# S5 maps: two products summed inside TensorE instead of on VectorE

## The chip, the cores and the metric

The kernel runs on one core of one Trainium2 chip. The metric is the device time of one execution in microseconds (us). The engines are TensorE (PE in the rows; its weight loads are PEld), VectorE (DVE), ScalarE (ACT), GpSimd (POOL) and the DMA queues, which SyncE (SP) issues for the most part. Each engine works through its own list of instructions in order and waits on semaphores for the others.

## The reference, cut to what matters

The program is one layer of an encoder: an S5 state-space mixer with GLU beside a cross-attention, an output projection with a layer norm, and a mixture of 16 experts. The change touches only the S5 mixer:

```
lam_bar = exp(lam * step)                                   # per direction, 32 groups x 64 states, complex
b_bar = ((lam_bar - 1.0) / lam)[..., None] * bmat
bu = einsum('blgc,gpc->blgp', ug, b_bar)                    # 16 channels of a group to 64 states
_, states = associative_scan(combine, (lam_bar, bu), reverse=(direction == 1), axis=1)
y = y + real(einsum('gcp,blgp->blgc', cmat, states))
```

The scan over 2048 steps is done in 128 chunks of 16 steps. For that the kernel needs, for each group and direction, an input map (16 steps x 16 channels to 64 complex states): its entries are real and imaginary parts of `lam_bar^k * b_bar`, k from 0 to 15, and an output map with `lam_bar^k * c`.

## The kernel before, in words

The part that matters runs from the start to about 333 us. In `inproj_u`, 16 tiles of 128 tokens are loaded and projected: for each tile t, `pu` (24 fp16 matmuls of 512 columns, the S5 input) and `pq` (48 fp16 matmuls of 128 columns, the query). Each of the two has one PSUM buffer; `pq` is read by ACT and DVE into `OT`. After the first tile, `s5_base` computes powers of `lam_bar` (`PR`, `PI`; `PRb` is the copy of `PR` in PSUM) and the products with b (`XB`, `YB`), mostly on DVE. `scan_base` builds a rotation table `E` on DVE and POOL. From tile 6 on, `s5_block(b)` makes the maps of 4 groups; there are 8 such blocks, and all of them come before the scans.

In `s5_block`, the helper `powers` makes one map of one direction from two products: POOL multiplies the imaginary parts into `wtmp` (two buffers), DVE multiplies the real parts into `wz` in PSUM (half a block at a time) and then adds both into `wi` (input map, one buffer) or `wo` (output map). The 16 tiles of `wi` in a block are transposed by TensorE with the identity into `ptw` (four to a PSUM tile, two tiles in rotation, shared with `ptu`), ACT copies them to `wt`, and a DMA stores `wt` in `wid`. After that `pkk` (fp32 matmuls of `wo` against `XB`) makes the convolution kernel `kd`. `ptu` are the transposes of the projected input into `U`.

At the end of the stage `chunk_inputs` multiplies `wt` and `U` (`pvv`) for the two last blocks, whose maps stay on the chip; ACT copies the result to `S`. Then `scan` turns the states (`m`, on DVE and POOL), scans them on DVE and turns them back, block by block, while `kv` prepares the cross-attention's keys. Later stages (attention, GLU, output projection, experts) are not touched.

No order is written out by hand here: a scheduler in the framework orders each engine's list from its own estimates, so an edit can also move instructions that it does not name. From `s5_out` on the order of TensorE alone is the one of the code. The lines to follow are 576 (POOL's product), 580 (DVE's product), 581 (DVE's sum), 600 (the transposes), 612 to 614 (`pkk`), 638 (`pvv`), 690 to 715 (the scan).

Of the kernel before, what the change touches and what calls it, by code (L numbers as in the profile page):

```python
# [9 lines left out]
F32 = mybir.dt.float32  # L10
# [3 lines left out]
ALU = mybir.AluOpType  # L14
# [4 lines left out]
P = 128  # L19
# [5 lines left out]
GB = 4  # L25
KEEP = 2
NB = G // GB
# [40 lines left out]
EPS2 = 1e-5 * GATE * GATE  # L68
EPS = 1e-5
MAGIC = 12582912.0  # L70


class Kern:
# [307 lines left out]
    def s5_base(self, t0):  # L381
# [13 lines left out]
        with ExitStack() as s:  # L395
# [9 lines left out]
            def ts(x, s1, op0, s2=None, op1=None, dt=F32):  # L405
                o = T("ts", dt)
                V.tensor_scalar(o, x, s1, s2, op0=op0, **({"op1": op1} if op1 is not None else {}))
                return o
# [13 lines left out]
            def rnd(x, k):  # L422
                return ts(ts(x, k, MUL, MAGIC, ADD), MAGIC, SUB)

# [126 lines left out]
    def s5_block(self, b, ps):  # L551
        nc = self.nc
        V, Q = nc.vector, nc.gpsimd
        bp = self.blkp
        gs = slice(b * GB, b * GB + GB)
        wo = bp.tile([P, GB, 2, 17, 16], F32, tag="wo", bufs=2, name=f"wo{b}")
        if b < NB - 1:
            wi = bp.tile([P, GB, 2, 16, 16], F32, tag="wi", bufs=1, name=f"wi{b}")
        else:
            wi = self.spare.rearrange("p a g d k -> p (a g d k)").rearrange("p (g d n c) -> p g d n c", g=GB, d=2, c=16)  # L560

        def pw(t, sl, d, q, n):
            t = t[:, sl, d, gs][:, :, q].rearrange("p n g -> p g n")
            return t.unsqueeze(3).to_broadcast([P, t.shape[1], n, 16])

        def ch(t, q, n):
            t = t[:, q]
            return t.unsqueeze(2).to_broadcast([P, t.shape[1], n, 16])


        def powers(o, x, y, d, n, back, nm):
            up = slice(n - 1, None, -1) if back else slice(0, n)
            lo = slice(n, 0, -1) if back else slice(1, n + 1)
            t = bp.tile([P, GB, 16, 16], F32, tag="wtmp", bufs=2, name=f"wtmp{nm}")
            all_ = slice(0, GB)
            Q.tensor_tensor(t[:, :, 0:n], ch(y, all_, n), pw(self.PI, lo, d, all_, n), op=ALU.mult)
            for h in range(2):
                q = slice(2 * h, 2 * h + 2)
                z = ps.tile([P, 2, 16, 16], F32, tag="wz", bufs=1, name=f"wz{nm}{h}")[:, :, 0:n]
                V.tensor_tensor(z, ch(x, q, n), pw(self.PRb, up, d, q, n), op=ALU.mult)  # L580
                V.tensor_tensor(o[:, q], z, t[:, q, 0:n], op=ALU.add)

        for d in range(2):
            o = wi[:, :, d]
            nc.scalar.activation(o[:, :, 15 if d == 0 else 0], self.XB[:, d, gs], AF.Copy)
            powers(o[:, :, 0:15] if d == 0 else o[:, :, 1:16], self.XB[:, d, gs], self.YB[:, d, gs], d, 15, d == 0, f"i{b}{d}")
        for d in range(2):
            o = wo[:, :, d]
            nc.scalar.activation(o[:, :, 16 if d == 0 else 0], self.XC[:, gs], AF.Copy)
            powers(o[:, :, 0:16] if d == 0 else o[:, :, 1:17], self.XC[:, gs], self.YC[:, gs], d, 16, d == 0, f"o{b}{d}")  # L590
        wof = wo.rearrange("p g d n c -> p g d (n c)")
        for d in range(2):
            nc.sync.dma_start(self.wod[b][:, :, d], wof[:, :, d, 16 * d:16 * d + 256])
        wt = bp.tile([P, GB, 2, 2, P], F32, tag="wt", bufs=2, name=f"wt{b}")
        for g in range(GB):
            pt = ps.tile([P, 512], F32, tag="tr", bufs=2, name=f"ptw{b}{g}")
            for d in range(2):
                for J in range(2):
                    q = d * 2 + J
                    nc.tensor.transpose(pt[:, q * P:q * P + P], wi[:, g, d, 8 * J:8 * J + 8].rearrange("p j c -> p (j c)"), self.ident)  # L600
            nc.scalar.activation(wt[:, g].rearrange("p d j s -> p (d j s)"), pt, AF.Copy)
        if b < NB - KEEP:
            nc.sync.dma_start(self.wid[b], wt)

        pk = ps.tile([P, 512], F32, tag="pk", bufs=1, name=f"pkk{b}")
        for g in range(GB):
            r = slice(g * 32, g * 32 + 32)
            gi = b * GB + g
            lf = self.XB[:, 0, gi:gi + 2, :].rearrange("p g c -> p (g c)")
            lb = self.XB[:, 1, gi:gi + 2, :].rearrange("p g c -> p (g c)")  # L610
            tp = (0, g * 32)
            nc.tensor.matmul(pk[r, 0:256], lf, wof[:, g, 0, 16:272], start=True, stop=False, tile_position=tp)
            nc.tensor.matmul(pk[r, 240:256], lb, wof[:, g, 1, 0:16], start=False, stop=True, tile_position=tp)
            nc.tensor.matmul(pk[r, 256:496], lb, wof[:, g, 1, 16:256], start=True, stop=True, tile_position=tp)
        ks = bp.tile([P, TAU * 16], F32, tag="ks", bufs=1, name=f"ks{b}")
        nc.scalar.activation(ks, pk[:, :496], AF.Copy)
        V.tensor_tensor(ks[:, 240:256], ks[:, 240:256], self.Dd[:, b], op=ALU.add)
        for g in range(GB):
            nc.sync.dma_start(self.kd[b][:, g], ks[g * 32:g * 32 + 16])
        return wt  # L620
# [547 lines left out]
    def list_row(self, kp, pos, e, out, shape, nm):  # L1168
# [3 lines left out]
        V.tensor_scalar(c, pos, 1.0 / P, -0.5 + 1.0 / 256, op0=ALU.mult, op1=ALU.add)  # L1172
        V.tensor_scalar(c, c, MAGIC, MAGIC, op0=ALU.add, op1=ALU.subtract)
        q = kp.tile([P] + shape, F32, tag=f"lr_q{shape[0]}", name=f"lrq{nm}")
# [6 lines left out]
    def overflow_tiles(self, c, n, nm):  # L1181
# [4 lines left out]
        V.tensor_scalar(nov, nov, 1.0 / OVT, (OVT - 1.0) / OVT - 0.5 + 1.0 / (2 * OVT), op0=ALU.mult, op1=ALU.add)  # L1186
        V.tensor_scalar(nov, nov, MAGIC, MAGIC, op0=ALU.add, op1=ALU.subtract)
        one = T([NE], "one")
# [414 lines left out]
```

## Time and profile before

| what | value |
|---|---|
| median of 3 runs | 1094.92 us (1094.09 to 1098.54) |
| the profiled execution | 1094.93 us, of which the span of its instructions is 1093.1 us |
| busy share of the span | PE 82%, DVE 79%, POOL 52%, ACT 49% |
| mean granted clock of TensorE | 0.927 of full speed |

The span runs from the first to the last instruction; 1.83 us of the profiled execution lie around it. Busy time of PE overlaps: a matmul is shown until its result has drained, while the next one already runs, so what a matmul costs in a row of equal ones is the distance from start to start. The chain that ended last covers only the last 12 us and says nothing of this stage.

### The profile page before, as it was taken

What the parts mean: (1) busy time and instruction counts of PE and PEld (TensorE: products, weight loads), DVE (VectorE), ACT (ScalarE), POOL (GpSimd) and SP (SyncE); (2) the same over time, 40 slices, a digit from 0 to 9 for tenths busy, and PEclk for the clock granted to TensorE, in tenths of its full rate; (3) what the DMA queues carried; (4) which work ended last, traced back from release to release, by engine and by line L of the source; (5) the groups of instructions that cost most, each with busy time, mean ns of one, the idle gap of its engine ahead of it and who ended that gap; (6) DMA issues with size and microseconds to landing.
All of it is one profiled execution on the core that took longest, in us unless ns stands there. A gap on an engine that the chain in (4) does not pass through costs nothing. (4 is left out here: it accounts for less than half of the span.)

```text
span 1093.1 us, 18792 instructions
## 1 busy us (share of the span) xinstructions
PE 900.1 (82%) x7108; PEld 606.2 (55%) x7108; DVE 861.1 (79%) x1704; ACT 533.3 (49%) x1052; POOL 568.9 (52%) x403
## 2 busy tenths in 40 slices
PE   7678599986736998899999888698969996989880
PEld 4445455665625777444455447486647664756640
DVE  7999988869999878983585767478858796879774
ACT  5123243444836666677733312276536564656530
POOL 1475754336656557425935444524524556357454
PEclk9899899998977999999999887899989998999995
DMA  7113355274271340417745331586578669567531
GB/s 254 39 57 107 117 199 183 78 256 144 69 222 58 119 143 10 140 54 261 253 149 115 80 117 59 172 327 220 181 249 294 223 220 326 188 218 237 211 104 65
DMA packets 65197, 178.13 MB, mean 163 GB/s; under 512 B 15120, under 2 KB 33424, under 8 KB 57680
## 3 DMA queue, kind: packets, MB, share of 16 engines
q1 hardware_dynamic: 44800, 128.83, 35.7%
q0 software_dynamic: 20304, 48.07, 12.9%
q8 instruction: 57, 0.93, 0.4%
q14 instruction: 36, 0.29, 0.1%
HBM read 141.95 MB, written 58.49 MB: 183 GB/s over the span
## 5 line engine op out<-in xcount | busy, mean ns | idle before, releaser
L92 DVE SCALAR_TENSOR_TENSOR wl<-raw,wh 128x1024 f16<-128x1024 f32 x82 | 97.7, 1217 | 9.7 <-ACT wh L91 9.7
L91 ACT ACTIVATE wh<-raw 128x1024 f16<-128x1024 f32 x82 | 81.9, 1048 | 24.3 <-PE pg L109 13.5
L109 PE MATMUL pg<-xl,wh 128*128 128x288 f16 (+1 forms) x256 | 72.9, 287 | 3.7 <-DVE xl L1473 3.6
L1217 POOL DMA_INDIRECT xs<-xg,idxall x31 | 40.8, 1317 | 67.3 <-DVE xg L1510 40.2
L108 PE MATMUL pg<-xh,wh 128*128 128x288 f16 (+1 forms) x256 | 73.1, 288 | 0.0
L110 PE MATMUL pg<-xh,wl 128*128 128x288 f16 (+1 forms) x256 | 72.7, 287 | 0.0
L108 PE MATMUL pu<-xh,wh 128*128 128x288 f16 (+1 forms) x256 | 71.3, 281 | 1.7 <-DVE hl L1060 1.7
L109 PE MATMUL pu<-xl,wh 128*128 128x288 f16 (+1 forms) x256 | 71.2, 281 | 0.0
L110 PE MATMUL pu<-xh,wl 128*128 128x288 f16 (+1 forms) x256 | 71.1, 281 | 0.0
L110 PEld LDWEIGHTS <-wl 128*128 128x128 f16 x576 | 57.7, 100 | 17.7 <-issue 4.5
L109 PEld LDWEIGHTS <-wh 128*128 128x128 f16 x576 | 57.8, 100 | 17.2 <-issue 3.8
L108 PEld LDWEIGHTS <-wh 128*128 128x128 f16 x576 | 58.0, 101 | 15.7 <-issue 0.9
L108 PE MATMUL pq<-xh,S 128*128 128x128 f16 x256 | 49.7, 232 | 17.8 <-DVE OT L295 17.8
L108 PE MATMUL py<-wh,hh 128*128 128x512 f16 x120 | 45.9, 385 | 14.0 <-DVE xg L1510 9.9
L108 PE MATMUL pu<-winh,xh 128*128 128x512 f16 x128 | 49.7, 389 | 6.8 <-ACT winh L91 6.8
L691 POOL TENSOR_TENSOR m<-S,R 128x1024 f32<-128x1024 f32 x10 | 33.0, 3301 | 42.4 <-DVE S L715 24.1
L1212 POOL DMA_INDIRECT xg<-x1d,idxall x31 | 36.9, 1191 | 32.9 <-DMA out_x<-xg,idxall 11.9
L1469 PE MATMUL pt<-ident,xg 128*128 128x128 f32 x240 | 37.9, 286 | 17.3 <-DVE xl L1473 7.9
L1473 DVE TENSOR_TENSOR xl<-pt,xh 128x512 f16<-128x512 f32 x60 | 39.5, 682 | 14.9 <-ACT xh L1472 14.9
L109 PE MATMUL pu<-winl,xh 128*128 128x512 f16 x128 | 49.7, 388 | 0.1
L1472 ACT ACTIVATE xh<-pt 128x512 f16<-128x512 f32 x60 | 33.9, 592 | 32.4 <-PE pt L1469 32.4
L110 PE MATMUL pq<-xh,S 128*128 128x128 f16 x256 | 49.7, 232 | 0.0
(476 smaller groups left out, 3205.6 us busy)
## 6 DMA issues: line engine op xcount, KB each, us to landing
raw<-in_w_gate SPq DMA_DIRECT2D x16, 1024.0 KB
raw<-in_w_up SPq DMA_DIRECT2D x16, 1024.0 KB
raw<-in_w_down SPq DMA_DIRECT2D x16, 1024.0 KB
xr<-in_xT SPq DMA_DIRECT2D x16, 512.0 KB
xs<-wo SPq DMA_DIRECT2D x16, 512.0 KB
wol<-xs SPq DMA_DIRECT2D x16, 512.0 KB
M<-kd SPq DMA_DIRECT2D x64, 128.0 KB
xres<-in_x SPq DMA_DIRECT2D x16, 512.0 KB
```

Of the source, the lines that this page charges most:

```text
L91: self.nc.scalar.activation(hi, raw, AF.Copy, scale=WS)
L92: self.nc.vector.scalar_tensor_tensor(lo, raw, WS, hi, op0=ALU.mult, op1=ALU.subtract)
L108: mm(ps, lh, rh, start=first, stop=False)
L109: mm(ps, lh, rl, start=False, stop=False)
L110: mm(ps, ll, rh, start=False, stop=last)
L691: Q.tensor_tensor(m[:, 1], S[:, :, 1::-1], tab(1), op=ALU.mult)
L1212: return self.nc.gpsimd.indirect_dma_start(out=out, out_offset=None, in_=src, in_offset=bass.IndirectOffsetOnAxis(ap=idx, axis=0))
L1217: st = self.nc.gpsimd.indirect_dma_start(out=self.xs, out_offset=bass.IndirectOffsetOnAxis(ap=si, axis=0), in_=z[:sz], in_offset=None, bou ...
L1469: nc.tensor.transpose(pt[:, i, off:off + sz], x[:sz, (d0 + i) * P:(d0 + i) * P + P], self.ident[:sz, :sz])
L1472: nc.scalar.activation(xh[:, ds_, :n], pt, AF.Copy)
L1473: nc.vector.tensor_tensor(xl[:, ds_, :n], pt, xh[:, ds_, :n], op=ALU.subtract)
```

## The change

The sum on VectorE and `wz` go for the input map only. DVE now multiplies the real parts of a whole block and direction straight into `wi` (line 590 in the new file), POOL multiplies the imaginary parts into a second buffer, and TensorE transposes both and adds them in PSUM: two fp32 matmuls with the identity as the moving operand, the first with `start`, the second with `stop`, take the place of each transpose. For blocks 0 to 5 the second buffer is a part of `U[:, 1]`, which is free until the last tile; blocks 6 and 7 use `wtmp`. POOL's product has 16 steps instead of 15. The output map is made as before.

```diff
+WTB = 2
...
-        for d in range(2):
             o = wi[:, :, d]
             nc.scalar.activation(o[:, :, 15 if d == 0 else 0], self.XB[:, d, gs], AF.Copy)
-            powers(o[:, :, 0:15] if d == 0 else o[:, :, 1:16], self.XB[:, d, gs], self.YB[:, d, gs], d, 15, d == 0, f"i{b}{d}")
+            V.tensor_tensor(o[:, :, 0:15] if d == 0 else o[:, :, 1:16], ch(self.XB[:, d, gs], all_, 15),
+                            pw(self.PRb, slice(14, None, -1) if d == 0 else slice(0, 15), d, all_, 15), op=ALU.mult)
+            if b < NB - 2:
+                t = self.U[:, 1, (b % 2 * 2 + d) * 8:(b % 2 * 2 + d) * 8 + 8].rearrange("p (g n) (m c) -> p g (n m) c", g=GB, c=16)
+            else:
+                t = bp.tile([P, GB, 16, 16], F32, tag="wtmp", bufs=WTB, name=f"wtmpi{b}{d}")
+            Q.tensor_tensor(t, ch(self.YB[:, d, gs], all_, 16),
+                            pw(self.PI, slice(15, None, -1) if d == 0 else slice(0, 16), d, all_, 16), op=ALU.mult)
+            wti.append(t)
...
-                    nc.tensor.transpose(pt[:, q * P:q * P + P], wi[:, g, d, 8 * J:8 * J + 8].rearrange("p j c -> p (j c)"), self.ident)
+                    for k, w in enumerate((wi[:, g, d], wti[d][:, g])):
+                        nc.tensor.matmul(pt[:, q * P:q * P + P], w[:, 8 * J:8 * J + 8].rearrange("p j c -> p (j c)"), self.ident,
+                                         start=(k == 0), stop=(k == 1))
```

The scheduler's lists change with it. On PE, where block 0's input map is turned (inside `pu` of tile 6), before:

```order
L108 LDWEIGHTS xh_1243
L108 MATMUL pu_1249<-winh,xh_1243 128x512
L600 MATMUL ptw_686<-ident,wi_646 128x128 x2
L600 MATMUL ptw_692<-ident,wi_646 128x128 x2
L109 LDWEIGHTS xh_1243
L109 MATMUL pu_1249<-winl,xh_1243 128x512
```

and now (line numbers are higher by 1 to 15 in the new file):

```order
L111 LDWEIGHTS xl_1256
L111 MATMUL pu_1261<-winh,xl_1256 128x512
L614 MATMUL ptw_674<-ident,wi_646 128x128
L614 MATMUL ptw_674<-ident,U 128x128
...
L614 MATMUL ptw_684<-ident,wi_646 128x128
L614 MATMUL ptw_684<-ident,U 128x128
...
L627 MATMUL pkk_715<-wo_645,XB 32x256
L628 MATMUL pkk_715<-wo_645,XB 32x16
```

A run of 16 plain matmuls stands where 4 transposes stood, after the whole of `pu` instead of inside it. In all, the list has 256 `ptw` matmuls where there were 128. The maps of blocks 0 to 2 are now turned before `ptu` and tile 8, and those of block 3 right behind them.

On DVE, at block 0's input map and the start of its output map, before:

```order
L581 TENSOR_TENSOR wi_646<-wzi_650,wtmpi_648 128x2x240
L580 TENSOR_TENSOR wzi_653<-XB,PRb 128x2x240
L295 SCALAR_TENSOR_TENSOR OT<-pq_1104,OT 64x2x128
L581 TENSOR_TENSOR wi_646<-wzi_653,wtmpi_648 128x2x240
L262 TENSOR_TENSOR xl_1391<-xr_1247,xh_1390 128x1024
L657 TENSOR_TENSOR S<-E 128x64
L580 TENSOR_TENSOR wzi_659<-XB,PRb 128x2x240
```

and now:

```order
L590 TENSOR_TENSOR wi_646<-XB,PRb 128x4x240 x2
L582 TENSOR_TENSOR wzo_656<-XC,PRb 128x512
L263 TENSOR_TENSOR xl_1403<-xr_1259,xh_1402 128x1024
L296 SCALAR_TENSOR_TENSOR OT<-pq_1112,OT 64x2x128
L583 TENSOR_TENSOR wo_645<-wzo_656,wtmpo_654 128x2x256
L582 TENSOR_TENSOR wzo_659<-XC,PRb 128x512
```

Eight instructions of a block became two of twice the length, and no sum of the input map is left. At the start of the scans DVE had before:

```order
L349 TENSOR_TENSOR meml<-mraw_2843,memh 128x1024
L349 TENSOR_TENSOR meml<-mraw_2847,memh 128x1024
L690 TENSOR_TENSOR m_2774<-S,R_2775 128x1024
L695 TENSOR_TENSOR S<-m_2774 128x2x256 x2
L715 SCALAR_TENSOR_TENSOR S<-decay,S 128x128 x4
```

and has now:

```order
L705 TENSOR_TENSOR m_2810<-S,R_2811 128x1024
L710 TENSOR_TENSOR S<-m_2810 128x2x256 x2
L730 SCALAR_TENSOR_TENSOR S<-decay,S 128x128 x8
L350 TENSOR_TENSOR meml<-mraw_2879,memh 128x1024
L705 TENSOR_TENSOR m_2810<-S,R_2811 128x1024
L350 TENSOR_TENSOR meml<-mraw_2883,memh 128x1024
```

The two conversions of the memory tokens (`meml`) moved from ahead of the first scan to behind it.

## Rows read from the trace of the kernel before

**Rows 1.** Page, busy time by engine: us, share of the span, instructions.
```profile
PE 900.1 (82%) x7108; PEld 606.2 (55%) x7108; DVE 861.1 (79%) x1704; ACT 533.3 (49%) x1052; POOL 568.9 (52%) x403
```

**Rows 2.** Windows: stretch, its length, busy us of each engine, granted clock, DMA share.
```profile
74.00:140.00 66.00, 48.98 (x443) 34.12 (x441) 61.23 (x89) 20.04 (x47) 43.30 (x26) 0.90 0.34 118
120.00:130.00 10.00, 6.56 (x61) 4.92 (x62) 8.47 (x12) 0.78 (x3) 7.52 (x4) 0.60 0.48 159
140.00:224.00 84.00, 82.12 (x665) 50.81 (x664) 70.34 (x105) 36.43 (x81) 38.23 (x19) 1.00 0.43 142
233.00:333.00 100.00, 61.67 (x566) 49.35 (x563) 96.31 (x118) 51.66 (x119) 60.70 (x24) 0.83 0.52 156
74.00:233.00 159.00, 138.90 (x1236) 92.19 (x1233) 137.55 (x197) 60.61 (x132) 84.14 (x48) 0.96 0.42 144
```

**Rows 3.** Waits of PE from 74 to 233 us: total, times, longest.
```profile
PE pkk L614 <- DVE wo L581: 8.1, 2, 7.3
PE pq L108 <- DVE OT L295: 4.1, 3, 2.4
PE pkk L612 <- DVE wo L581: 2.5, 1, 2.5
PE ptw L600 <- DVE wi L581: 2.3, 2, 1.8
```

**Rows 4.** Groups by form on DVE and POOL: busy us, mean ns | idle before.
```profile
L580 DVE TENSOR_TENSOR wzo<-XC,PRb 128x512 f32<-128x512 f32 x32 | 22.2, 693 | 0.8
L580 DVE TENSOR_TENSOR wzi<-XB,PRb 128x480 f32<-128x480 f32 x32 | 21.1, 659 | 0.7
L581 DVE TENSOR_TENSOR wi<-wzi,wtmpi 128x480 f32<-128x480 f32 x28 | 18.4, 656 | 3.1 <-POOL wtmpi L576 1.8
L581 DVE TENSOR_TENSOR S<-wzi,wtmpi 128x480 f32<-128x480 f32 x4 | 2.6, 655 | 0.2
L576 POOL TENSOR_TENSOR wtmpo<-YC,PI 128x1024 f32<-128x1024 f32 x16 | 33.8, 2114 | 27.6 <-DVE wi L581 22.1 <-DVE ks L617 2.8 <-DVE S L581 2.7
L576 POOL TENSOR_TENSOR wtmpi<-YB,PI 128x960 f32<-128x960 f32 x16 | 31.8, 1988 | 19.5 <-DVE wo L581 19.5
```

**Rows 5.** Groups by form on PE, 74 to 233 us.
```profile
L612 PE MATMUL pkk<-wo,XB 128*32 128x256 f32 x64 | 19.4, 406 | 2.6 <-DVE wo L581 2.5
L600 PE MATMUL ptw<-ident,wi 128*128 128x128 f32 x112 | 17.1, 279 | 3.3 <-DVE wi L581 2.3 <-ACT wt L601 0.8 <-ACT U L306 0.2
L638 PE MATMUL pvv<-U,wt 128*64 128x128 f32 x128 | 7.4, 274 | 1.2 <-ACT S L641 1.2
L600 PE MATMUL ptw<-ident,S 128*128 128x128 f32 x16 | 2.1, 276 | 0.0
```

**Rows 6.** Timeline of PE: start, length in us, instruction.
```profile
166.58 1.04 PE L600 MATMUL ptw<-ident,wi 128*128 128x128 f32 x8
167.55 0.62 PE L612 MATMUL pkk<-wo,XB 128*32 128x256 f32 x2
...
293.27 0.59 PE L808 MATMUL py<-wol,SS 128*128 128x256 f32 x2
293.70 0.59 PE L809 MATMUL py<-wol,SS 128*128 128x256 f32 x2
...
660.76 1.93 PE L966 MATMUL pl<-wr,xT 128*128 128x20 f32 x16 [0.51 <-DVE lg L972]
```

**Rows 7.** Timeline of DVE at the start of the scans.
```profile
228.92 1.23 DVE L349 TENSOR_TENSOR meml<-mraw,memh 128x1024 f16<-128x1024 f32 x1
230.06 3.38 DVE L690 TENSOR_TENSOR m<-S,R 128x1024 f32<-128x1024 f32 x1
...
238.55 1.22 DVE L690 TENSOR_TENSOR m<-S,R 128x1024 f32<-128x1024 f32 x1
242.03 0.69 DVE L695 TENSOR_TENSOR S<-m 128x512 f32<-128x512 f32 x1 [2.25 <-POOL m L691]
243.88 1.23 DVE L690 TENSOR_TENSOR m<-S,R 128x1024 f32<-128x1024 f32 x1 [1.16 <-POOL S L695]
```

**Rows 8.** Timeline of ACT at the end of the stage.
```profile
228.79 1.07 ACT L641 ACTIVATE S<-pvv 128x512 f32<-128x512 f32 x2
```

More of the change, by code (lines that the diff above doesn't have):

```diff
@@ L560, in s5_block @@
             wi = self.spare.rearrange("p a g d k -> p (a g d k)").rearrange("p (g d n c) -> p g d n c", g=GB, d=2, c=16)
+        all_ = slice(0, GB)
         def pw(t, sl, d, q, n):
@@ L573, in powers @@
             lo = slice(n, 0, -1) if back else slice(1, n + 1)
-            t = bp.tile([P, GB, 16, 16], F32, tag="wtmp", bufs=2, name=f"wtmp{nm}")
-            all_ = slice(0, GB)
+            t = bp.tile([P, GB, 16, 16], F32, tag="wtmp", bufs=WTB, name=f"wtmp{nm}")
             Q.tensor_tensor(t[:, :, 0:n], ch(y, all_, n), pw(self.PI, lo, d, all_, n), op=ALU.mult)
@@ L581, in powers @@
                 V.tensor_tensor(o[:, q], z, t[:, q, 0:n], op=ALU.add)
+        wti = []
         for d in range(2):
```

## The prediction

> **What bounds the kernel now.** I read the page's busy shares first: PE 82% and DVE 79% of the span [rows 1] are two near-equal averages, and neither says who ends the stage that the change touches. The windows do. Between 74 and 140 us (tile 6 onwards, blocks 0 to 2, the rotation table) DVE is busy 61.2 of 66 us and PE 49.0; between 140 and 224 us (blocks 3 to 7, tiles 8 to 15) PE is busy 82.1 of 84 us and DVE 70.3; from 233 to 333 us (the scans) DVE is busy 96.3 of 100 us and PE 61.7 [rows 2]. So the limit changes hands twice: DVE, then PE, then DVE. What the change is worth is read between 74 us, where tile 6 begins on PE, and 233 us, where `pvv` of the two last blocks ends; the scans can't begin before `pvv`. In these 159 us PE works 138.9 us and stands idle 20.1 [rows 2]. 17.0 of the 20.1 are four waits for DVE: 8.1 and 2.5 us of `pkk` for `wo`, 4.1 of `pq` for `OT`, 2.3 of `ptw` for `wi` [rows 3]; a `pkk` wait of 7.3 us lies in the slow stretch around 120 us, where the granted clock was 0.60.
>
> **DVE's part.** Removed: 32 products of 480 elements at 659 ns and 32 sums at 656 ns (28 and 4), 21.1 + 18.4 + 2.6 = 42.1 us. Added: 16 products of 960. 480 elements take 659 ns and 512 take 693 [rows 4], 1.06 ns an element, so 960 take 0.659 + 480 x 1.06 ns = 1.17 us, 18.7 us in all. DVE saves 23.4 us, 2.9 us a block. It counts where PE waits for DVE, up to about 140 us, and nowhere behind that.
>
> **POOL's part.** 16 products grow from 1988 to the 2114 ns of the 1024-element form, +2.0 us [rows 4]. POOL has 43.3 of 66 and 38.2 of 84 us of work [rows 2], and its waits for DVE to release `wtmp` get fewer, since the input map of blocks 0 to 5 has buffers of its own in `U`. I cost it at nothing; POOL's 2 us is its price if that cover fails. ACT's and the DMA queue's work is the same in amount. Token loads now stand behind stores of earlier blocks on SP's queue, but blocks 0 to 3 themselves come earlier against the tiles, so the loads of tiles 9 and later, issued when those stores are ready, land tens of us before their tile: nothing.
>
> **PE's part, the term that decides.** Removed: 128 transposes (112 + 16 in rows 5). Eight in a row take 0.97 us from start to the next instruction's start [rows 6], 0.121 us each: 15.5 us. Added: 256 plain fp32 matmuls of 128 columns. The trace of before has this operation with other sizes, and its counts tell something that the code doesn't: the code issues 64 `pvv` matmuls for the two last blocks, 32 `pkk` matmuls of line 612 and 128 transposes, and the trace has 128, 64 and 128 of them [rows 5]. A plain fp32 matmul runs as two passes, a transpose as one. So 512 passes come in. What a pass costs is bounded by two rows: two `py` passes of 256 columns take 0.43 us from start to start, 0.84 ns a column, which makes 0.1075 us of 128; and the router's fp32 passes with a full 128x128 weight and only 20 columns still take 1.93 us for 16, 0.121 us each [rows 6], so loading an fp32 weight sets a floor of the same size, hidden behind the pass before it. I take 0.115 us: 58.9 us (55.0 to 62.0). Net on PE: +43.4 us (39.5 to 46.5).
>
> The Trainium skill, in "TensorE: Matmul & The Clock Gate", section Terms, says that the transpose mode is four times faster for FP32. By that a plain matmul would cost four transposes instead of the 1.9 (0.23 against 0.121 us) of these rows; what that would give is the third rival.
>
> **What lies beside other work.** The idle 20.1 us of PE are the only room. They shrink from both sides: a block's maps are ready 2.9 us earlier on DVE, and PE has 5.4 us more to do in each block (43.4 / 8), so a wait for `wo` of 7.3 us is closed by one block. But they don't go to zero. The scheduler now puts the maps of blocks 0 to 2 one behind the other into tiles 6 and 7, where PE has little else to do when DVE is late; and in blocks 6 and 7 POOL's products for both maps share the two `wtmp` buffers, which now stay taken until PE has turned the input map, so that POOL (2.1 us) and DVE (0.7 us each) come after it and before the last `pkk`, which stands ahead of `pvv`. A new wait of PE for DVE holds up `pq`, `pu` and with them everything behind. I leave 7 us of idle time (0 to 17): 13.1 us are recovered. The clock: a denser PE should not fall to 0.60 as between 120 and 130 us, where 6.6 us of work were done [rows 2]; at full clock that work is at best 3.3 us shorter; I take 2.
>
> **The start of the scans.** DVE begins at 230.06 us, 0.2 us after ACT has written `S` (228.79 + 1.07) [rows 7, 8]. It will begin right behind `S` again, that much later. The two `meml` (1.23 us each) were done before it for free and now fall behind the first scan, into waits of 2.25 and 1.16 us for POOL [rows 7]: they cost what they fill. In before they also stood ahead of `S` through ACT's part of them; I take 1 us of gain (0 to 1.5). After that DVE is the limit with the same work and everything later shifts as a whole.
>
> **The sum.** +43.4 (passes) - 13.1 (idle time filled) - 2 (clock) - 1 (start of the scans) = +27.3 us. Against the profiled execution, 1094.93 us (span 1093.1 and 1.83 around it), that is 1122 us; the median of the runs shown is 1094.92, so nothing is to be corrected. Lower end: 39.5 - 20.1 - 3.3 - 1.5 = +14.6, 1109.5 us. Upper end: 46.5 - 3.1 - 0 - 0 = +43.4, 1138 us.
>
> **Rivals.**
> 1. Faster or no change: PE takes the extra work within its waits, and DVE's 23.4 us decide. This needs one pass a matmul when the moving operand is the identity. Then 256 x 0.115 = 29.4 us come in, net +13.9; less 13.1 to 20.1 of idle time, 2 of clock and 1 of the scans, that is -2 to -9, 1086 to 1093 us. For it: DVE is the limit up to 140 us and gives up 2.9 us a block. Against it: all three plain fp32 groups have two records a matmul, whatever their operands. The point from which it decides: net cost on PE below 16 us, that is under 0.25 us for what one transpose did; I expect 0.46.
> 2. Much slower through waits: DVE and POOL can't feed PE in the early blocks, or the one buffer of `wi`, now held through 7.4 us of matmuls, makes DVE wait and then PE again for `OT`. Idle time stays at the 17 to 22 us of today: +43.4 - 3 to + 2, 1135 to 1140 us. For it: DVE is 93% busy in that stretch. Against it: DVE loses a fifth of its work there and PE gains it.
> 3. The passes cost four transposes: 256 x 0.484 = 124 us, net +108, less 20 of idle time and 3 of clock and scans: +85, 1180 us. Against it: every row of fp32 passes is at 0.11 to 0.12 us.
> 4. The shift is partly given back behind 233 us, by another order of the scans, the keys and the attention, which the scheduler also moved: 10 to 15 us less, 1107 to 1112 us. Against it: DVE is 96% busy there, with the same work.
>
> **Chances.** Forecast 80%, rival 1 6%, rival 2 8%, rival 3 2%, rival 4 4%. The forecast's own range is 1110 to 1135. For 8 in 10 I take 1108 to 1137, which holds rival 4 and half of rival 2 and leaves out rivals 1 and 3. About 0.5% (5.5 us) is what a measurement of this kernel can tell from no change. Rival 1 splits evenly between faster and the same, and a little more is left for an early stage that goes better than counted: faster 4%, same 5%, slower 91%.
>
> **What would show it.** Right: 512 records of `ptw` with some 0.115 us from start to start; `pvv` ending at 256 to 264 us instead of 233; PE busy above 95% of the time from 74 us on, and DVE at some 70%; DVE's groups of 480 elements replaced by 16 of 1.17 us; the distance from the first `m` to the end as before, within 5 us. Wrong: 256 records of `ptw`, or a pitch over 0.13 us; PE waiting more than 17 us for DVE before `pvv`; or `pvv` late by 25 us and the end not.

## The result and the profile after

The changed kernel takes 1134.24 us (1126.02 to 1136.3, 4 runs) against 1095.87 for the kernel before on the same chip (1094.09 to 1098.54): a ratio of 1.0336 [1.0297, 1.0375]. On a second chip it was 1.0350 [1.0307, 1.0393]. The forecast was 1122 us within 1108 to 1137: slower, inside the range near its upper end, and some 10 us short. The profiled execution has a span of 1130.6 us against 1093.1, +37.5 us, and these 37.5 are what the forecast's +27.3 is held against.

The page, busy time by engine (answers to [rows 1]):

```profile
PE 943.0 (83%) x7492; PEld 654.4 (58%) x7492; DVE 840.8 (74%) x1656; ACT 534.6 (47%) x1052; POOL 574.6 (51%) x403
```

PE has 384 records more, which is 512 passes less 128 transposes. DVE works 20.3 us less in the whole execution.

Windows of the changed kernel, with the columns of [rows 2]:

```profile
74.00:140.00 66.00, 55.90 (x451) 42.09 (x449) 64.79 (x77) 19.50 (x48) 51.99 (x32) 0.97 0.35 118
120.00:130.00 10.00, 9.39 (x102) 7.90 (x103) 9.90 (x10) 2.86 (x9) 7.91 (x5) 1.00 0.55 208
140.00:224.00 84.00, 83.39 (x751) 62.46 (x750) 34.79 (x51) 28.55 (x60) 17.36 (x9) 0.98 0.33 112
74.00:256.36 182.36, 170.09 (x1482) 128.06 (x1480) 114.88 (x150) 59.65 (x132) 81.39 (x47) 0.98 0.31 104
262.00:370.00 108.00, 64.55 (x602) 53.27 (x598) 97.61 (x122) 54.70 (x125) 63.86 (x26) 0.79 0.50 159
```

The fourth row ends where the first `pvv` begins on PE (256.36 us). The same row of the kernel before, up to its own first `pvv` (224.51 us):

```profile
74.00:224.51 150.51, 131.61 (x1108) 85.24 (x1105) 131.57 (x193) 56.93 (x127) 81.53 (x45) 0.95 0.39 132
```

From 74 us to the first `pvv` PE works 170.09 instead of 131.61 us, 38.5 more, and stands idle 12.3 instead of 18.9 us, 6.6 less. The idle time that is left lies mostly before 140 us (66 - 55.90 = 10.1 us), where DVE is busier than before (64.8 of 66 us against 61.2): DVE now makes the input maps of blocks 0 to 3 in this stretch, where it made those of blocks 0 to 2 before, and it is still the limit there. From 140 us to the first `pvv` PE is idle for only 2.2 of 116.4 us.

Waits of PE from 74 to 262 us (total, times, longest; answers to [rows 3]):

```profile
PE ptw L614 <- DVE wi L590: 4.1, 2, 3.0
PE pkk L627 <- DVE wo L583: 4.0, 2, 3.5
PE pkk L629 <- DVE wo L583: 2.9, 3, 2.0
PE ptu L302 <- DVE U L305: 1.2, 2, 0.7
```

Groups by form on PE and DVE (answers to [rows 4, 5]): busy us, mean ns | idle before.

```profile
L614 PE MATMUL ptw<-ident,wi 128*128 128x128 f32 x224 | 44.8, 283 | 4.1 <-DVE wi L590 4.1
L614 PE MATMUL ptw<-ident,U 128*128 128x128 f32 x192 | 38.0, 281 | 0.0
L614 PE MATMUL ptw<-ident,wtmpi 128*128 128x128 f32 x64 | 12.4, 277 | 0.0
L614 PE MATMUL ptw<-ident,S 128*128 128x128 f32 x32 | 6.1, 277 | 0.0
L590 DVE TENSOR_TENSOR wi<-XB,PRb 128x960 f32<-128x960 f32 x14 | 15.5, 1148 | 13.0 <-PE ptw L614 13.0
```

224 + 192 + 64 + 32 = 512 records for 256 matmuls. What one costs is read from start to start, on PE's timeline (start, length; answers to [rows 6]):

```profile
121.96 0.39 PE L614 MATMUL ptw<-ident,U 128*128 128x128 f32 x2
122.18 0.39 PE L614 MATMUL ptw<-ident,wi 128*128 128x128 f32 x2
...
125.08 0.39 PE L614 MATMUL ptw<-ident,U 128*128 128x128 f32 x2
```

Fourteen matmuls lie between the first and the last of these starts: 3.12 / 14 = 0.223 us each, 0.111 us a pass. Where a transpose cost 0.121 us, the two matmuls in its place cost 0.446.

The start of the scans on DVE (answers to [rows 7]):

```profile
257.08 0.68 DVE L583 TENSOR_TENSOR wo<-wzo,wtmpo 128x512 f32<-128x512 f32 x1
260.92 0.18 DVE L632 TENSOR_TENSOR ks<-ks,Dd 128x16 f32<-128x16 f32 x1 [3.16 <-ACT ks L631]
262.12 1.23 DVE L705 TENSOR_TENSOR m<-S,R 128x1024 f32<-128x1024 f32 x1 [1.02 <-ACT S L656]
265.59 1.29 DVE L710 TENSOR_TENSOR S<-m 128x512 f32<-128x512 f32 x2 [2.24 <-POOL m L706]
266.80 2.63 DVE L730 TENSOR_TENSOR_SCAN S<-decay,S 128x128 f32<-128x128 f32 x8
269.34 1.20 DVE L350 TENSOR_TENSOR meml<-mraw,memh 128x1024 f16<-128x1024 f32 x1
270.45 1.22 DVE L705 TENSOR_TENSOR m<-S,R 128x1024 f32<-128x1024 f32 x1
271.59 1.22 DVE L350 TENSOR_TENSOR meml<-mraw,memh 128x1024 f16<-128x1024 f32 x1
275.05 0.69 DVE L710 TENSOR_TENSOR S<-m 128x512 f32<-128x512 f32 x1 [2.24 <-POOL m L706]
...
361.36 0.66 DVE L93 SCALAR_TENSOR_TENSOR E<-E 128x512 f16<-128x512 f32 x1
...
363.23 1.86 DVE L93 SCALAR_TENSOR_TENSOR E<-E 128x512 f16<-128x512 f32 x3
...
370.26 1.47 DVE L837 COPY S<-trg 128x512 f32<-128x512 f32 x2
```

The first `m` starts at 262.12 us, 32.1 later than before. It follows ACT's second copy of `pvv` into `S` directly, and that copy needs 64 records of `pvv`. Block 7 stands among them: its last `wo` ends at 257.76, and its `pkk` take 1.0 us between two runs of `pvv`. PE's first `pvv` before, PE's timeline there now, and ACT's second copy:

```profile
224.51 3.71 PE L638 MATMUL pvv<-U,wt 128*64 128x128 f32 x64
...
256.36 2.83 PE L653 MATMUL pvv<-U,wt 128*64 128x128 f32 x46
259.12 0.39 PE L629 MATMUL pkk<-wo,XB 128*32 128x240 f32 x1
...
260.15 4.80 PE L653 MATMUL pvv<-U,wt 128*64 128x128 f32 x82
...
261.49 0.60 ACT L656 ACTIVATE S<-pvv 128x512 f32<-128x512 f32 x1 [0.60 <-PE pvv L653]
```

Three marks split every trace: the first `pvv` on PE, the first `m` on DVE, and the first copy of `trg` on DVE, which stands at the end of the scans (331.06 us before; one last product of the scans is still behind it there). "Stage" is from `m` to `trg`, "rest" from `trg` to the end of the span.

| kernel | span | `pvv` | `m` | stage | rest | PE idle, 74 us to `pvv` |
|---|---|---|---|---|---|---|
| before | 1093.1 | 224.5 | 230.1 | 101.0 | 762.0 | 18.9 |
| after | 1130.6 | 256.4 | 262.1 | 108.1 | 760.3 | 12.3 |

The 37.5 us are 31.9 to the first `pvv`, 0.2 from there to `m`, 7.1 in the stage and -1.7 in the rest.

### The profile page after: what moved, and what is told of

Same layout as the page of the kernel before. It is cut to its first block, busy times and chain, and to the rows that moved or that the text cites. A ratio compares the mean times of both kernels' runs of the same rounds, so it can differ in the third digit from the quotient of the medians.

```text
span 1130.6 us, 19492 instructions
## 1 busy us (share of the span) xinstructions
PE 943.0 (83%) x7492; PEld 654.4 (58%) x7492; DVE 840.8 (74%) x1656; ACT 534.6 (47%) x1052; POOL 574.6 (51%) x403
## 5 line engine op out<-in xcount | busy, mean ns | idle before, releaser
L1232 POOL DMA_INDIRECT xs<-xg,idxall x31 | 37.3, 1203 | 72.7 <-DVE xg L1525 30.1
L578 POOL TENSOR_TENSOR wtmpo<-YC,PI 128x1024 f32<-128x1024 f32 x16 | 33.2, 2082 | 70.3 <-PE ptw L614 51.8
L109 PE MATMUL pq<-xh,S 128*128 128x128 f16 x256 | 49.3, 232 | 11.3 <-DVE OT L296 11.3
L1484 PE MATMUL pt<-ident,xg 128*128 128x128 f32 x240 | 39.5, 289 | 18.9 <-DMA xg<-x1d,idxall 14.9
L1525 DVE SCALAR_TENSOR_TENSOR xg<-py,idxall,xg 128x512 f32<-128x512 f32 x60 | 43.5, 744 | 11.1 <-DMA xg<-xs,idxall 8.3
L111 PE MATMUL pu<-winh,xl 128*128 128x512 f16 x128 | 49.5, 387 | 0.6 <-POOL xl L263 0.6
L1488 DVE TENSOR_TENSOR xl<-pt,xh 128x512 f16<-128x512 f32 x60 | 40.4, 685 | 12.2 <-ACT xh L1487 11.5
```

The lines of the kernel that those rows point to most:

```text
L109: mm(ps, lh, rh, start=first, stop=False)
L111: mm(ps, ll, rh, start=False, stop=last)
L1232: st = self.nc.gpsimd.indirect_dma_start(out=self.xs, out_offset=bass.IndirectOffsetOnAxis(ap=si, axis=0), in_=z[:sz], in_offset=None, bou ...
L1484: nc.tensor.transpose(pt[:, i, off:off + sz], x[:sz, (d0 + i) * P:(d0 + i) * P + P], self.ident[:sz, :sz])
L1488: nc.vector.tensor_tensor(xl[:, ds_, :n], pt, xh[:, ds_, :n], op=ALU.subtract)
L1525: nc.vector.scalar_tensor_tensor(xg[:sz, hs], py[:sz], gate, xg[:sz, hs], op0=ALU.mult, op1=ALU.add, **acc)
```

## The experiments

The theory from here: each pass stands on the path at its full price of 0.11 us, the waits of PE for DVE shrink only as far as DVE's own relief goes, and the scans lose some microseconds by their order. The rivals: PE hides part of the passes in its waits (then a pass costs less than its pitch); or the new buffers and the scheduler's other order, not the passes, make the loss; or the loss in the scans comes from PE's load.

**Two transposes in place of two matmuls** (the second overwrites the first, so the map lacks the real product). The order of the changed kernel, with 256 transposes of one pass each instead of 512 passes.

```diff
-                    for k, w in enumerate((wi[:, g, d], wti[d][:, g])):
-                        nc.tensor.matmul(pt[...], w[...], self.ident, start=(k == 0), stop=(k == 1))
+                    for w in (wi[:, g, d], wti[d][:, g]):
+                        nc.tensor.transpose(pt[...], w[...], self.ident)
```

> The changed kernel with two transposes in place of the two matmuls (the second overwrites the first, nothing is added): 256 passes of 0.121 us. Theory A: +15.5 us on PE, DVE 23 us lighter, so pvv ends at 228 to 242 us instead of 264; with the same order of the scans as the changed kernel some 7 us more there: 1095 to 1110 us. Theory B: everything but the price of a pass is as in the changed kernel, hence 1125 to 1136 us.

Measured: 1.0070 [1.0039, 1.0101]; `m` at 236.5 us, stage 107.5. So 256 passes fewer bring `m` 25.6 us forward, against 26.1 by the distances from start to start (512 x 0.1114 less 256 x 0.121), and the stage stays as long as in the changed kernel: its loss does not come from the passes.

**One matmul of the two** (the imaginary product is made but left out of the sum).

```diff
-                    for k, w in enumerate((wi[:, g, d], wti[d][:, g])):
-                        nc.tensor.matmul(pt[...], w[...], self.ident, start=(k == 0), stop=(k == 1))
+                    nc.tensor.matmul(pt[...], wi[:, g, d][...], self.ident, start=True, stop=True)
```

> The changed kernel with the second matmul of each tile left out (the imaginary product is made and not added): 128 plain fp32 matmuls, 256 passes, DVE as in the changed kernel. Theory A, PE's passes decide: 256 x 0.112 - 15.5 = +13.2 us on PE against the kernel before, to be absorbed by its 20 us of idle time as DVE is 23 us lighter; 1088 to 1100 us, pvv of the last blocks ending at 226 to 240 us. Theory B, bunched blocks and the new order cost the time and not the passes: as the changed kernel, 1125 to 1136 us, as far as the order stays the same.

Measured: 0.9995 [0.9963, 1.0026]; `m` at 233.0, stage 102.1. DVE's relief and 128 passes more nearly cancel: `m` is 2.9 us later than in the kernel before.

**Three matmuls** (the imaginary product is added twice).

```diff
-                    for k, w in enumerate((wi[:, g, d], wti[d][:, g])):
+                    for k, w in enumerate((wi[:, g, d], wti[d][:, g], wti[d][:, g])):
...
-                                         start=(k == 0), stop=(k == 1))
+                                         start=(k == 0), stop=(k == 2))
```

> The changed kernel with a third matmul on each tile (the imaginary product is added twice): 768 passes. Theory A: PE has no idle time left, so 256 more passes cost nearly their full 256 x 0.112 = 28.7 us: 1157 to 1168 us. Theory B: 1134 to 1142 us.

Measured: 1.0548 [1.0485, 1.0611], 1155.64 us, a little under what was expected; `m` at 289.3, 27.2 us behind the changed kernel for 256 passes, 0.106 us each. Its window from 74 us to the first `pvv`:

```profile
74.00:284.93 210.93, 200.10 (x1750) 158.65 (x1747) 115.05 (x152) 60.54 (x133) 80.62 (x48) 0.98 0.27 92
```

210.93 - 200.10 = 10.8 us idle, 1.5 us less than in the changed kernel, whose second profile has 10.7 itself: another 256 passes fill no waits that these profiles can tell.

**The kernel before with plain matmuls** in place of its transposes; everything else as before.

```diff
-                    nc.tensor.transpose(pt[...], wi[...], self.ident)
+                    nc.tensor.matmul(pt[...], wi[...], self.ident, start=True, stop=True)
```

> The kernel before with each transpose written as a plain fp32 matmul with the identity; VectorE's sum stays. Theory A: 256 records of ptw instead of 128, +13.2 us of PE work; DVE is as busy as before, so part of PE's waits stays: +3 to +13 us, 1099 to 1109 us. Theory B: no new buffers, no bunching, hence 1093 to 1098 us.

Measured: 1.0139 [1.0079, 1.0199], 1113.67 us, above the expectation. `m` comes 11.0 us later (0.086 a pass), as expected of 128 passes of which a part falls into waits (PE's idle time up to the first `pvv` is 16.3 us against 18.9); but 1.9 us more in the stage and 7.0 in the rest of the one profiled execution have no cause that I found.

**DVE's relief alone**: the changed kernel with one transpose of `wi` as before (the imaginary product is made but left out of the sum). PE has the work of before, DVE that of the changed kernel.

```diff
-                    for k, w in enumerate((wi[:, g, d], wti[d][:, g])):
-                        nc.tensor.matmul(pt[...], w[...], self.ident, start=(k == 0), stop=(k == 1))
+                    nc.tensor.transpose(pt[...], wi[:, g, d][...], self.ident)
```

> The imaginary product is made and left out of the sum; wi is turned by 128 transposes as before. DVE has 23.4 us less to do, PE the same as in the kernel before: the saving without its price. Theory A: PE's waits for DVE up to 140 us go, 8 to 14 us: 1082 to 1090 us. Rival, DVE's sums lie beside other work: 1094 to 1099 us.

Measured: 0.9919 [0.9887, 0.9952]; `m` at 219.6, 10.5 us before that of the kernel before. Its window up to the first `pvv`:

```profile
74.00:214.91 140.91, 129.73 (x1109) 84.18 (x1106) 119.04 (x153) 57.37 (x133) 82.81 (x49) 0.98 0.43 142
```

140.91 - 129.73 = 11.2 us idle. The idle time of PE falls from 18.9 to 11.2 us by DVE's relief, and then stays, however much PE is given, in the four kernels that have this relief in all blocks: 11.2 here with no pass added, 10.9 with 128 (one matmul), 12.3 with 384 (the change), 10.8 with 640 (three matmuls). The relief, together with the new buffers and the new order, is worth 10.5 us at `m`, and each pass added costs its full price: from this kernel to one matmul 13.4 us for 128 (0.105), from there to the change 29.2 for 256 (0.114). -10.5 + 384 x 0.11 = +31.7 against the +32.1 measured at `m`. The medians follow within their few microseconds of scatter, that of the change with the 7.1 us of its stage on top.

**All eight blocks' second products in `U`**: blocks 6 and 7 no longer share `wtmp`.

```diff
-            if b < NB - 2:
+            if b < NB:
```

> The changed kernel, but POOL's product of blocks 6 and 7 goes to U as well, not to wtmp; the 512 passes stay. In the changed kernel DVE begins the scans 32 us later than before and the stage of the scans is 7 us longer. Theory A: the 32 us are PE's passes, the 7 us come from block 7's end (its output map waits for wtmp, its stores hold the loads of the keys behind them, and DVE's splitting of the keys' weights moves out of the waits for POOL): first m at 256 to 262 us, scans 101 to 104 us, 1122 to 1130 us. Rival: the 7 us are contention that any denser start brings: scans 106 to 109 us, 1131 to 1138 us.

Measured: 1.0338 [1.0281, 1.0394]. The stage is 100.8 us, as expected and as before the change (one of its four `kvl`, part of the keys' weights, now stands ahead of `m`); `m` is at 265.5, 3.4 us later than in the changed kernel, where an earlier one was expected. Both ran once more, side by side:

> The changed kernel once more, beside the version with all of POOL's products in U on the same chip. Theory A: ratio 1.030 to 1.038 to the kernel before, scans of 107 to 109 us from the first m to the first trg copy.

> All of POOL's products of the input map in U, once more, beside the changed kernel on the same chip. The first look had scans 7 us shorter and a first m 3 us later than the changed kernel, and the same ratio on another chip. Theory A: the order of the scans is worth what the later m leaves of it: 3 to 6 us less than the changed kernel. Rival: it is taken back elsewhere: within 2 us of it.

Measured: the changed kernel 1.0350 [1.0307, 1.0393], the variant 1.0367 [1.0325, 1.0408]: no difference in the time, though the marks repeat to 0.2 us (stages 108.0 and 100.8, `m` at 262.0 and 265.4). Of the 7 us by which its stage is shorter, 3.4 are lost ahead of `m`, and the rest does not show within intervals of 4 us either way. The variant's DVE timeline at the start of the scans shows the other order:

```profile
264.33 1.23 DVE L93 SCALAR_TENSOR_TENSOR kvl<-kraw,kvh 128x1024 f16<-128x1024 f32 x1 [2.90 <-ACT kvh L92]
265.48 3.38 DVE L705 TENSOR_TENSOR m<-S,R 128x1024 f32<-128x1024 f32 x1
268.96 1.29 DVE L710 TENSOR_TENSOR S<-m 128x512 f32<-128x512 f32 x2
```

No `meml` behind the first scan, and no `E<-E` (2.5 us, part of the gate's weights) ahead of `trg`. Over all traces this sorts the stages. Both stand inside in the changed kernel (108.1, 108.0), with two transposes (107.5) and with three matmuls (105.4); neither in the rest, whose stages are 98.0 to 102.9.

**The sum on PE in blocks 0 and 1 only**, where DVE is the limit; blocks 2 to 7 as before.

```diff
+PESUM = 2
...
+            if b >= PESUM:
+                powers(o[...], self.XB[:, d, gs], self.YB[:, d, gs], d, 15, d == 0, f"i{b}{d}")
+                continue
...
+                    if b >= PESUM:
+                        nc.tensor.transpose(pt[...], wi[...], self.ident)
+                        continue
```

> PE's sum for blocks 0 and 1 only, blocks 2 to 7 as in the kernel before. PE gets 2 x 5.2 = 10.4 us more, DVE 5.8 us less, both in the stretch where PE of the kernel before waits 17 us for DVE. Theory A: the passes disappear in those waits: 1091 to 1100 us. Rival (a plain matmul costs its full time wherever it stands): +10 us, 1105 to 1109 us.

Measured: 0.9980 [0.9954, 1.0006], not told apart from the kernel before, as expected of passes that disappear. The order of the scans is a good one (stage 98.0). `m` is at 228.4, 1.6 us earlier than in the kernel before, although 96 passes are added. Its window to 226 us (the first `pvv` begins at 224.03):

```profile
74.00:226.00 152.00, 140.26 (x1240) 96.42 (x1239) 130.39 (x192) 60.46 (x135) 79.98 (x47) 0.99 0.42 145
```

152 - 140.26 = 11.7 us idle, as little as with the relief of all eight blocks. A reckoning by blocks fails here: a quarter of the 10.5 us, less 96 passes at 0.11 (10.6 us), would put `m` 8 us later than in the kernel before. Either the relief of the first two blocks is worth nearly all of the 10.5 us, or these passes fell into waits; no run has the relief of two blocks without the passes, so this stays open.

**POOL adds for blocks 0 to 2**, PE transposes as before.

```diff
+POOLSUM = 3
...
+            V.tensor_tensor(oo, ch(self.XB[:, d, gs], all_, 15), pw(self.PRb, ...), op=ALU.mult)
+            Q.tensor_tensor(t, ch(self.YB[:, d, gs], all_, 15), pw(self.PI, ...), op=ALU.mult)
+            Q.tensor_tensor(oo, oo, t, op=ALU.add)
```

> Transposes as in the kernel before; in blocks 0 to 2 DVE makes one product per direction and POOL adds (6 sums of some 2.0 us more on POOL), blocks 3 to 7 as before. Theory A: DVE is the limit up to 140 us and gives up 8.8 us, PE gets nothing: 1087 to 1095 us. Rival: POOL, with 43 of 66 us of work there, becomes late with the rotation table and its products: 1098 to 1106 us.

Measured: 1.0001 [0.9972, 1.0031]: nothing gained. POOL's work from 74 us to the first `pvv` rises from 81.5 to 93.9 us, PE's idle time falls only from 18.9 to 16.0, and `m` comes 1.0 us earlier (229.0).

**PE for blocks 0 and 1, POOL for block 2**: the two edits above together.

```diff
+            if b == PESUM:
...
+                Q.tensor_tensor(oo, oo, t, op=ALU.add)
+                continue
```

> PE's sum for blocks 0 and 1, POOL's sum for block 2 (two sums of some 2 us), blocks 3 to 7 as before. The version with PE's sum in two blocks came out at 0.998 of before; there PE is busy from 140 us on without a gap and in 56 of 66 us before. Theory A: DVE gives up another 2.9 us before 140 us and PE gets nothing more: 2 to 6 us faster than the kernel before, ratio 0.994 to 0.998. Rival: PE is the limit throughout by now, DVE's relief is worth nothing more: as with two blocks alone, 0.997 to 1.001.

Measured: 0.9996 [0.9975, 1.0017], as the rival had it; `m` is at 231.5, 1.4 us later than in the kernel before. No version that makes the whole sum is told apart as faster than the kernel before; the 0.9919 above leaves out the sum and shows what the idea would bring if the sum cost PE nothing.

**The buffers alone**: the kernel before, with POOL's product of the input map of blocks 0 to 5 in `U`.

```diff
-            t = bp.tile([P, GB, 16, 16], F32, tag="wtmp", bufs=WTB, name=f"wtmp{nm}")
+            if n == 15 and b < NB - 2:
+                t = self.U[:, 1, ...]
+            else:
+                t = bp.tile([P, GB, 16, 16], F32, tag="wtmp", bufs=WTB, name=f"wtmp{nm}")
```

> The kernel before with POOL's product of the input map of blocks 0 to 5 in U, VectorE's sums and the transposes as before: the change's buffers alone. Theory A, only DVE's load and PE's passes count: no change, ratio 0.996 to 1.004. Rival, part of what DVE's relief brought in the kernel without a sum was POOL running ahead: 3 to 8 us faster, ratio 0.993 to 0.997.

Measured: 1.0062 [1.0031, 1.0093], `m` 4.5 us later. The buffers, with the order that the scheduler makes of them, bring no gain by themselves but cost 0.6%. They can't be the loss of the changed kernel, since DVE's relief alone has the same buffers and is 0.8% faster; what they cost there is contained in its 10.5 us and not separated. Windows of this kernel:

```profile
110.00:120.00 10.00, 5.75 (x47) 3.87 (x44) 9.94 (x14) 2.81 (x6) 6.29 (x5) 0.68 0.34 131
120.00:130.00 10.00, 5.30 (x42) 3.87 (x40) 9.88 (x11) 1.36 (x4) 9.71 (x6) 0.50 0.43 139
130.00:140.00 10.00, 7.19 (x59) 6.43 (x57) 9.57 (x16) 2.25 (x7) 4.22 (x4) 0.67 0.03 7
```

From 120 to 130 us the granted clock is 0.50, the lower level of 1.2 GHz throughout, where the kernel before had 0.60 and the changed one 1.00; PE had been idle for 4.3 of the 10 us ahead of it. That is a place where the 4.5 us can lie; that they lie there was not tried.

## Why the prediction was right

The mechanism and the sign were right, and so was the main term; sizes behind it were off, and the two largest errors, the idle time and the stage, went the same way. That the time lies in the range is owed to the range's width: the sum alone missed 10.2 of 37.5 us.

| step | forecast | measured, us | from |
|---|---|---|---|
| passes less transposes | +43.4 | +41.5 | 512 x 0.1114 - 15.5 |
| clock, and overlap in PE's busy time | -2 | -3.0 | 38.5 - 41.5 |
| idle time of PE filled | -13.1 | -6.6 | 12.3 - 18.9 |
| start of the scans, `pvv` to `m` | -1 | +0.2 | 5.76 - 5.55 |
| the stage | 0 | +7.1 | 108.1 - 101.0 |
| the rest | 0 | -1.7 | 760.3 - 762.0 |
| sum | +27.3 | +37.5 | |

1. The passes. Two records a matmul and 0.111 us a pass, against a forecast of two and 0.115. Reading the number of passes from the counts of other fp32 groups decided the case. The 512 records refute the first rival, whose condition was one pass a matmul; the run with one matmul of the two, 256 passes, shows what that would have given (0.9995). The floor of 0.121 us that the prediction read from the router's 16 passes was the length of the whole row, drain included, and not a distance of starts; `ptw` goes below it with a weight load for each pass. The third, four transposes a matmul, needs 0.48 us and has 0.223, which is 1.84 transposes. For the factor of four that the Trainium skill ("TensorE: Matmul & The Clock Gate", Terms) gives to the transpose mode in FP32, read as a plain matmul against a transpose, the trace does not agree: it has 1.84.
2. The clock. The slow stretch went (0.60 to 1.00 at 120 to 130 us), as forecast. The 3.0 us are a difference of busy sums and hold more than the clock; they are not measured by themselves.
3. The idle time is, with the stage, the term most mis-sized. The step said that waits shrink from both sides, by DVE's relief and by PE's added work. The relief alone takes 7.7 of the 18.9 us, and PE's work on top of it takes nothing: 0, 128, 384 or 640 added passes leave 11 to 12 us. (Without the relief, 128 passes fill 2.6 us.) The remaining waits lie mostly before 140 us, where DVE is 90 to 98% busy in the four kernels with the relief. That each new piece of PE's work there only stands behind the same piece of DVE's is how I read this; no run tests it by itself, and the run with the sum on PE in two blocks can be read the other way. The sum counted 13.1 us as filled where 6.6 were, 6.5 of the 10.2 us missed.
4. The start of the scans gave nothing back. `m` follows `S` directly, as forecast (ACT's second copy ends at 262.09). But from the first `pvv` to `m` it takes 5.76 us instead of 5.55, since block 7's last `pkk` stand among the `pvv` for 1.0 us, and PE goes back to `pvv` only at 260.15. The cause is the chain that the prediction named: POOL's product for the output map comes after PE has turned the input map (POOL waits 51.8 us for `ptw` before `wtmpo`). Its price was put under the idle time, as a wait ahead of `pvv`; there PE's `pkk` wait only 0.9 us for `wo` behind 140 us.
5. "After that DVE is the limit with the same work and everything later shifts as a whole" failed in the stage. Its work there was not the same: `meml` (2.4 us) and `E<-E` (2.5) stand inside it, 4.9 of the 7.1 us; the other 2.2 us have no cause that is shown here. The step that failed said that `meml` falls "into waits of 2.25 and 1.16 us for POOL" and costs what it fills. It does not fill them. POOL's timeline at the two `meml`:

```profile
262.17 3.39 POOL L706 TENSOR_TENSOR m<-S,R 128x1024 f32<-128x1024 f32 x1 [11.21 <-ACT S L656]
...
269.57 5.45 POOL L706 TENSOR_TENSOR m<-S,R 128x1024 f32<-128x1024 f32 x1 [3.85 <-DVE S L730]
```

POOL's `m` takes 5.45 us beside DVE's `m` and `meml` and 3.39 beside `m` alone: it ends 2.1 us later, and DVE waits its 2.24 us all the same. `E<-E` in turn is work that came from behind `trg`, so a part of the 7.1 is only moved; the rest is 1.7 us shorter in this execution (1.6 longer in the second profile), and the variant without the long stage is no faster in its median. The distance from `m` to the end grew by 5.4 us against the 5 that the forecast allowed, and its runs scatter by more (868.5 and 871.5 us in two profiles of the same kernel). Over all traces the rest lies between 754.1 and 769.0 us, and no run shows why.
6. The second rival gave 1135 to 1140 us, near what came, by unchanged waits of 17 to 22 us. 12.3 us were left; a time near a rival's is no sign of its mechanism. Part of that mechanism did appear: DVE waits 13.0 us for PE to release `wi`, but all of it behind 140 us, where PE is the limit. The argument against it, that DVE loses a fifth of its work up to 140 us, was too high: three blocks of 2.9 us are a seventh of 61.2. The fourth, a part given back behind 233 us, did not come: the stage took 7.1 more.

Of the other signs: `pvv` ended at 264.95 us (256 to 264 forecast); DVE's products take 1.15 us (1.17); from 74 us to the first `pvv` PE is busy 93% of the time, not above 95%, and DVE 63%, not some 70%; PE's waits for DVE there come to 12.2 us, below the 17 that would have spoken against the forecast.

## What to carry to other kernels

Count records against instructions in the trace before: that a plain fp32 matmul shows twice and a transpose once decides what an accumulation on TensorE costs. Ask of an engine's idle time which engine makes it: here the relief of the late engine took 7.7 us of it, and 128 to 640 passes added to the waiting engine after that took nothing, so idle time can't be counted as room before it is known what each piece of the new work waits for. And before calling a move into a wait free, see whether the engine waited for is slowed by what is put there.

## What the runs showed of the hardware

DVE and POOL take turns on elementwise work of the kind shown here, with two operands in SBUF. A pair of `m`, one on each, takes 3.4 to 3.5 us whichever starts first: where POOL began first, in the kernel before, POOL takes 2.43 us and DVE 3.38 [rows 7]; in the changed kernel DVE takes 1.23 and POOL 3.39. POOL's row before:

```profile
229.94 2.43 POOL L691 TENSOR_TENSOR m<-S,R 128x1024 f32<-128x1024 f32 x1 [17.42 <-ACT S L641]
```

`kvl` takes 1.20 us alone and 3.36 beside POOL's `m`, as these rows of DVE after the change show:

```profile
284.25 1.23 DVE L705 TENSOR_TENSOR m<-S,R 128x1024 f32<-128x1024 f32 x1
285.39 3.36 DVE L93 SCALAR_TENSOR_TENSOR kvl<-kraw,kvh 128x1024 f16<-128x1024 f32 x1
...
298.62 1.20 DVE L93 SCALAR_TENSOR_TENSOR kvl<-kraw,kvh 128x1024 f16<-128x1024 f32 x1
```

The Trainium skill ("SBUF — State Buffer", SBUF: two separate sides) says that the two share a port pair as an exclusive lock, which a DVE instruction with two SBUF inputs and a GpSimd instruction hold for their whole length. By that rule a `meml` in a wait for POOL costs its full 1.2 us, and the trace agrees: with two of them beside it POOL's `m` takes 5.45 instead of 3.39 us.

An fp32 pass of 128 columns costs 0.111 us from start to start at full clock (granted clock 1.00), and 0.105 to 0.114 us of the kernel's way to the first `m` where DVE is relieved (0.086 where it is not); a transpose of the same tile is one pass of 0.121.
